# A hybrid attention and DeltaNet layer: the order of attention pieces, and which PSUM banks the middle projections use

## The chip, the cores and the metric

The kernel runs on one core of one Trainium2 chip. Its engines are TensorE (PE, with the weight loads PEld shown apart), VectorE (DVE), ScalarE (ACT), GpSimd (POOL) and SyncE (SP), whose queue issues all the DMAs here. The metric is the device time of one execution in microseconds (us). Shown are the median of several runs and, apart from them, one execution that was profiled.

## The reference

One layer of an encoder for 1024 tokens of width 1024, in float32:

```python
h = rms_norm(x, g_mix_pre);  proj = h @ w_in
aq, ak, av, dqkv, dgate, dalpha, dbeta = split(proj)
attn_o = window_attention(rope(aq), rope(ak), av, sink)   # 8 heads, 2 kv heads, blocks of 128, +-128 tokens
dn_o   = gated_deltanet(dqkv, dgate, dalpha, dbeta)       # 4 heads of 128, two directions, gated per-head norm
x = x + rms_norm(concat(attn_o, dn_o) @ w_out, g_mix_post)
c = cross_attention(rms_norm(x, g_cross_pre), rms_norm(mem, g_mem), w_cq, w_ckv, w_co)  # 4 heads of 256, 256 memory tokens
x = x + rms_norm(c, g_cross_post)
x = x + rms_norm(swiglu(rms_norm(x, g_ffn_pre), w_gate_up, w_down), g_ffn_post)
```

The chunked delta rule is a recurrence over the sequence; the kernel walks it in 8 steps of 128 tokens, for both directions at once.

## The kernel before, in words

Large products are made of three matmuls: each operand is split (`split`, L100) into a rounded part, written by ScalarE (L103), and a remainder, written by VectorE or GpSimd (L104), and the product of the two remainders is left out. Weights come through the pool `wp`: a load into `wraw`, then `whi` and `wlo`, each with two buffers (`load_w`, L119).

A planner orders the instructions of each engine when the program is built. It takes the program's order as priority, simulates the engines, and at each moment puts in what is ready; `load_w` raises its priority by 300 instructions (`AHEAD`). Tiles of one name in a pool share that name's buffers and get them in the order in which the program asks. On the chip each engine works through its list in the planned order, and so does the SP queue.

The mixer is written out as three lists of letters that `issue` (L729) walks.
- `ORDER_1` makes the DeltaNet's queries, keys and values and what the scans need of them.
- `ORDER_2` (L38) makes the rest: `L` are the last levels of the triangular inverses, `A` the attention projections, `V` the attention values, `G` the gate projections (`gate_proj`, L777), `W` calls `next_windows`.
- `ORDER_3` (L39): `M` normalises the memory tokens (`memory_norm`, L917), `s01` is one step of the scans of both head pairs (`scan`, L795), `K` one of eight column blocks of the memory keys (`next_keys`, L941), `V` one half of the memory values.

The window attention is cut into 16 pieces, one per block of 128 queries and kv group g (`window`, L632); pieces 0 to 7 belong to group 0. The first half of a piece makes four heads' scores on the PSUM tiles `psw`, the softmax, and the normalised probabilities `sc`. The second half transposes them (`ptw`) and multiplies by the values (`pow`). Both draw on two banks of the pool `pw`. One call of `next_windows` (L703) begins two pieces and finishes the two begun before them; nine calls make all 16. With the first piece of a group it calls `window_keys` (L696), which loads that group's keys into a `wraw` buffer (`kraw`) and splits them into `khi` (two buffers) and `klo` (one buffer).

The scans, the memory norm (`ptm`), the memory keys (`pck`) and the memory values (`pcv`) share the five PSUM banks of the pool `pc` (L792). The memory norm loads its two tiles `mt` into `wraw` buffers, and uses `whi` buffers (`mjk`) for the squares.

After the mixer, PSUM is three pools: `pg3` with four banks, `pn3` and `px3` with two each (L995 to L997). `mid_gemm` (L1034) multiplies 512 tokens by a 1024x1024 matrix, in two halves of 512 columns; each half is four tiles of 128 tokens, one bank each, and four blocks of the inner dimension. A bank is read out by ScalarE (L1055, the square sum) and VectorE (L1056, times the gain). At its end it adds the residual, stores the sum, and scales it by its own inverse root mean square into `xr` (L1072) for the next norm, whose transposes are `ptn`. It is called four times: twice for `w_out` (L1095, L1097) and twice for `w_co` (L1183, L1197), once per half of the tokens.

Between them stand the query projections (`cross_q`, tiles `pcq` in `pg3`) and the cross attention (`cross_attention`, L1121), once per token half. For each of four heads it makes scores `pcs` in two tiles of `px3`, their maxima and exponentials, transposes `pct` in `pn3`, and the product with the values `pco` in two tiles of `px3`, whose result replaces the queries. `w_co` then multiplies that result.

Of the kernel before, what the change touches and what calls it, by code (L numbers as in the profile page):

```python
# [13 lines left out]
AF = mybir.ActivationFunctionType  # L14
ALU = mybir.AluOpType
# [8 lines left out]
NT = S // P  # L24
# [10 lines left out]


ORDER_1 = ("k0 k1 E0 K0 U0 E1 K1 U1 S0 q0 v0 q1 C0 v1 E2 C1 k2 E3 k3 q2 K2 U2 v2 K3 U3 S1 q3 C2 v3 C3 B0 B1").split()
ORDER_2 = "L0 L1 A4 V A0 A1 G0 G1 L2 L3 W W W A2 A3 G2 G3 W".split()  # L38
ORDER_3 = ("M " + "s01 W K " * 5 + "s01 K " * 3 + "s01 V V").split()  # L39


_NAMES = ["ident", "mUi", "mLi", "m5", "m6", "band0", "band1", "band2", "mU", "mL", "ones"]
# [34 lines left out]
def tile_hybrid_block(  # L77
# [6 lines left out]
    nc = tc.nc  # L84
    x, mem, out = x[0], mem[0], out[0]
    w_in, w_out, w_cq, w_ckv, w_co = w_in[0], w_out[0], w_cq[0], w_ckv[0], w_co[0]
# [100 lines left out]
    d_x1 = dram.tile([S, D], F32, name="d_x1")  # L187
    d_x2 = dram.tile([S, D], F32, name="d_x2")
# [443 lines left out]
    def window(n, g):  # L632

        tok = slice(n * P, (n + 1) * P)
        k0, k1 = max(n - 1, 0), min(n + 1, NT - 1) + 1
        nb = k1 - k0
        w = nb * P
        band = C[:, _AT["band0"] - C0 + (k0 - n + 1) * P:][:, 0:w]

        khi, klo = (t[:, k0 * P:k1 * P] for t in keys[g])  # L640
        qr = tw.tile([P, 4, P], F32, tag="qr", name="qr", bufs=1)
        for r in range(2):
            nc.sync.dma_start(qr[64 * r:64 * r + 64], d_q[256 * g:256 * g + 256, tok].rearrange("(h e) t -> e h t", h=4))
        qs = tw.tile([P, 4, P], F32R, tag="qs", name="qs")
        nc.scalar.copy(qs, qr)
        nc.gpsimd.tensor_tensor(qs[64:128], qr[64:128], f32(qs[64:128]), ALU.subtract)

        m4 = tw.tile([P, 4], F32, tag="m4", name="m4")
        ssum = tw.tile([P, 4], F32, tag="ssum", name="ssum")
        pr = []  # L650
        for hh in range(4):
            pp = pw.tile([P, 512], F32, tag="pw", name="psw")
            for i, kk in enumerate((khi, klo)):
                nc.tensor.matmul(pp[:, 0:w], qs[:, hh, :], kk, start=(i == 0), stop=(i == 1))
            sc = tw.tile([P, 384], F32, tag="sc", name="sc", bufs=8)
            nc.vector.tensor_tensor_reduce(out=sc[:, 0:w], in0=pp[:, 0:w], in1=band, scale=0.125,
                                           scalar=sink[:, 4 * g + hh:4 * g + hh + 1], op0=ALU.add, op1=ALU.max,
                                           accum_out=m4[:, hh:hh + 1])
            pr.append(sc)
        nm = tw.tile([P, 4], F32, tag="nm", name="nm")  # L660
        nc.vector.tensor_scalar(nm, m4, -1.0, None, ALU.mult)
        for hh in range(4):
            nc.scalar.activation(pr[hh][:, 0:w], pr[hh][:, 0:w], AF.Exp, bias=nm[:, hh:hh + 1],
                                 accum_out=ssum[:, hh:hh + 1])
        es = tw.tile([P, 4], F32, tag="es", name="es")
        nc.gpsimd.tensor_tensor(es, sink[:, 4 * g:4 * g + 4], m4, ALU.subtract)
        nc.scalar.activation(es, es, AF.Exp)
        nc.vector.tensor_tensor(es, es, ssum, ALU.add)
        nc.vector.reciprocal(es, es)
        for hh in range(4):  # L670
            if g * NT + n < 8:
                nc.vector.tensor_scalar(pr[hh][:, 0:w], pr[hh][:, 0:w], es[:, hh:hh + 1], None, ALU.mult)
            else:
                nc.scalar.mul(pr[hh][:, 0:w], pr[hh][:, 0:w], es[:, hh:hh + 1])
        yield
        po = pw.tile([P, 4, P], F32, tag="pow", name="pow", bufs=1)
        for j in range(nb):
            pp = pw.tile([P, 512], F32, tag="pw", name="ptw")
            for hh in range(4):
                nc.tensor.transpose(pp[:, hh * P:(hh + 1) * P], pr[hh][:, j * P:(j + 1) * P], ident)  # L680
            ph = tw.tile([P, 512], F32R, tag="ph", name="ph")
            pl = tw.tile([P, 512], F32R, tag="pl", name="pl")
            split(ph, pl, pp)
            for i, pe_ in enumerate((ph, pl)):
                nc.tensor.matmul(po.rearrange("p h t -> p (h t)"), vhl[:, k0 + j, g].rearrange("p r e -> p (r e)"), pe_,
                                 start=(j == 0 and i == 0), stop=(j == nb - 1 and i == 1))
        ao = tw.tile([P, 4, P], F32, tag="ao", name="ao", bufs=1)[0:64]
        nc.scalar.copy(ao, po[64:128])
        nc.vector.tensor_tensor(ao, po[0:64], ao, ALU.add)
        nc.sync.dma_start(d_mix[g * 256:(g + 1) * 256, tok].rearrange("(h e) t -> e h t", e=64), ao)  # L690
# [307 lines left out]
    L0 = ExitStack()  # L998
# [14 lines left out]
    def turn_norm(xn, gname, his, los, pin=False):  # L1013

        for k in range(KT):
            pt = pn.tile([P, 512], F32, tag="pn", name="ptn")
            for j in range(4):
                t = nc.tensor.transpose(pt[:, j * P:(j + 1) * P], xn[j][:, k * P:(k + 1) * P], ident)
                if pin and k + j == 0:
                    tc.keep_in_program_order(t)  # L1020
            split(his[:, k, :], los[:, k, :], pt, gain(gname, k))
# [9 lines left out]

    PG, PN, PX = (pg, "pg"), (pn, "pn"), (px, "px")

    def mid_gemm(tz, act, w, gp, res, dst, hf, between=None, banks=([PG] * 4, [PX] * 2 + [PG] * 2)):  # L1034


        zs = [tz.tile([P, D], F32, tag="z", name="z", bufs=4) for _ in range(4)]
        sss = [tz.tile([P, 2], F32, tag="zss", name="zss", bufs=8) for _ in range(4)]
        for ch in range(2):
            cs = slice(ch * 512, (ch + 1) * 512)  # L1040
            if ch and between:
                between()

            pp = [q_.tile([P, 512], F32, tag=t_, name="pmg") for q_, t_ in banks[ch]]
            for kp in range(4):
                whi, wlo = load_w(w[kp * 256:(kp + 1) * 256, cs], 2, 512)
                for t in range(4):
                    tt = slice(t * P, (t + 1) * P)
                    for kk in range(2):
                        k = 2 * kp + kk  # L1050
                        for i, (w_, a) in enumerate(((whi, 0), (whi, 1), (wlo, 0))):
                            nc.tensor.matmul(pp[t], act[a][:, k, tt], w_[:, kk, :], start=(k == 0 and i == 0),  # L1052
                                             stop=(k == KT - 1 and i == 2))
            for t in range(4):
                nc.scalar.activation(zs[t][:, cs], pp[t], AF.Square, accum_out=sss[t][:, ch:ch + 1])  # L1055
                nc.vector.tensor_tensor(zs[t][:, cs], pp[t], gp[:, cs], ALU.mult)  # L1056
        xn = []
        for t in range(4):
            tok = slice(hf * HALF + t * P, hf * HALF + (t + 1) * P)
            z = zs[t]  # L1060
            xr = tz.tile([P, D], F32, tag="xr", name="xr", bufs=XR)
            nc.sync.dma_start(xr, res[tok, :])
            rs = tz.tile([P, 1], F32, tag="prs", name="prs", bufs=4)
            nc.gpsimd.tensor_scalar(rs, sss[t][:, 1:2], sss[t][:, 0:1], D * EPS, ALU.add, ALU.add)
            nc.gpsimd.tensor_tensor(rs, rs, mhalf[:, 0:1], ALU.pow)
            nc.vector.scalar_tensor_tensor(z, z, rs, xr, ALU.mult, ALU.add)
            nc.sync.dma_start(dst[tok, :], z)
            s2 = tz.tile([P, 1], F32, tag="ps2", name="ps2", bufs=4)
            nc.scalar.activation(xr, z, AF.Square, accum_out=s2)
            r2 = tz.tile([P, 1], F32, tag="pr2", name="pr2", bufs=4)  # L1070
            rstd_of(r2, s2, 1.0 / D, EPS)
            nc.vector.tensor_scalar(xr, z, r2, None, ALU.mult)  # L1072
            xn.append(xr)
        return xn

# [4 lines left out]
    L1 = ExitStack()  # L1080
# [11 lines left out]
                              .rearrange("(k p) t -> p k t", p=P))  # L1092
            split(mxT[hf][0][:, k2, :], mxT[hf][1][:, k2, :], raw[:, k2, :])
    LR.close()
    xn0 = mid_gemm(tz, mxT[0], w_out, gp, x, d_x1, 0, banks=([PG] * 4, [PX] * 2 + [PN] * 2))  # L1095
    h2T = [[opB.tile([P, KT, HALF], F32R, tag=b1, name=b1), opB_first[2]]]
    xn1 = mid_gemm(tz, mxT[1], w_out, gp, x, d_x1, 1, between=lambda: turn_norm(xn0, "cross", *h2T[0], pin=True))  # L1097
    h2T.append(operand(opA, "s0"))
    turn_norm(xn1, "cross", *h2T[1])

# [92 lines left out]
    for k in range(KT):  # L1193
        pt = turned_k(xn, k)
        nc.scalar.activation(raw[:, k, :], pt, AF.Identity, scale=gain("ffn", k))
        split(x1h[:, k, :], x1l[:, k, :], raw[:, k, :], eng=nc.gpsimd)
    xn = mid_gemm(tz, q1, w_co, gp, d_x1, d_x2, 1)  # L1197
    T2, T4 = (blocks(t) for t in operand(opB, "s1"))
    T1, T3 = (blocks(t) for t in operand(opB, "s2"))
    for k in range(HK):  # L1200
# [355 lines left out]
```

## Time and profile before

| what | value |
|---|---|
| median of 3 runs | 1556.27 us (1555.42 to 1558.12) |
| the profiled execution's own time | 1553.82 us |
| its span, first to last instruction | 1551.8 us |
| mean granted TensorE clock | 0.992 |
| scans, memory keys, window pieces | about 290 to 574 us of the span |
| `w_out` products, cross attention, `w_co` products | about 550 to 903 us |

The profile is of one execution. A row of the timeline gives start and length in us, engine, line, operation, written and read tiles, shapes and count; in square brackets stands how long the engine was idle before and what ended that. A row of a group gives the total, a mean in ns, and the idle time before the group with what ended it. A row of a tile's view gives durations (min/median/max in ns) and the first and last start. Rows of windows are explained where they stand.

### The profile page before, as it was taken

The page shows a single profiled execution, that of the slowest core. Times are in us where ns is not written, and L with a number is a line of the kernel's source. Part 1 is how long each engine was busy: PE and PEld are TensorE (multiplying, and loading weights), DVE is VectorE, ACT ScalarE, POOL GpSimd, SP SyncE. Part 2 cuts the span into 40 slices and gives each one's busy share as a digit, 9 for nine tenths or more (in the row PEclk, how much of TensorE's full clock was granted, in tenths as well). Part 3 has the DMA queues.
Part 4 walks back from the last instruction along what each step waited for, and adds up shares of the span by engine and source line. Part 5 has one row for each costly group of instructions (what it writes and reads, how often), then busy time and mean ns, then how long its engine had stood idle before and what let it go on. Part 6 is the DMA issues. An engine that isn't in the chain of part 4 may idle for free.

```text
span 1551.8 us, 21044 instructions
## 1 busy us (share of the span) xinstructions
PE 1488.0 (96%) x7451; PEld 1248.9 (80%) x7451; DVE 1074.3 (69%) x1728; ACT 740.3 (48%) x1522; POOL 379.9 (24%) x364
## 2 busy tenths in 40 slices
PE   6999999998999999999987999999999999999997
PEld 5888888787989788888876887888888888888786
DVE  6868999686888766643444577776867554696665
ACT  5578732557467764443333664332323332354532
POOL 2020210111256103433000531443433432000021
PEclk9999999999999999999999999999999999999999
DMA  6244575856996755542210554344433334853354
GB/s 205 75 117 136 158 189 158 190 173 187 328 303 210 246 196 180 179 155 77 68 41 27 188 192 144 116 128 129 156 118 113 105 106 150 290 188 98 102 175 164
DMA packets 264710, 242.95 MB, mean 157 GB/s; under 512 B 33800, under 2 KB 203677, under 8 KB 264605
## 3 DMA queue, kind: packets, MB, share of 16 engines
q1 hardware_dynamic: 264605, 241.62, 50.0%
q8 instruction: 58, 0.95, 0.3%
q14 instruction: 47, 0.39, 0.1%
HBM read 172.07 MB, written 66.88 MB: 154 GB/s over the span
## 4 chain that ended last, share of the span: by engine, by line
PE 70%; DVE 7%; DMA 5%; ACT 5%; issue 2%; SPq 1%; POOL 1%; DVEq 0%; POOLq 0%; ACTq 0%
PE pmg L1052 11%; PE pD L1227 8%; PE pE L1227 8%; PE pA L1227 7%; PE pdX L1417 6%; PE pcq L261 5%; PE pdA L1417 4%; PE pB L1227 4%; PE psc L809 3%; PE pg L261 3%; PE pdD L1417 2%; PE pco L1159 2%; PE pcs L1133 2%; PE pck L949 1%; PE pdX L1510 1%
## 5 line engine op out<-in xcount | busy, mean ns | idle before, releaser
L103 ACT CAST whi<-wraw 128x1024 fp32r<-128x1024 f32 x108 | 113.6, 1052 | 176.6 <-PE pmg L1052 50.1
L261 PE MATMUL pg<-hlo,whi 128*128 128x512 f32 x352 | 139.7, 397 | 0.0
L261 PE MATMUL pg<-hhi,whi 128*128 128x512 f32 x352 | 139.3, 396 | 0.0
L261 PE MATMUL pg<-hhi,wlo 128*128 128x512 f32 x352 | 138.8, 395 | 0.0
L104 POOL TENSOR_TENSOR wlo<-wraw,whi 128x1024 fp32r<-128x1024 f32 x38 | 92.5, 2435 | 184.1 <-ACT whi L103 176.6
L104 DVE TENSOR_TENSOR wlo<-wraw,whi 128x1024 fp32r<-128x1024 f32 x70 | 87.1, 1245 | 71.9 <-ACT whi L103 64.4
L1052 PE MATMUL pmg<-whi,b 128*128 128x512 f32 x384 | 117.0, 393 | 1.1 <-DVE b L104 0.9
L1227 PE MATMUL pA<-s,whi 128*128 128x512 f32 x352 | 109.3, 392 | 1.0 <-ACT m L1244 1.0
L1052 PEld LDWEIGHTS pmg<-whi,b 128*128 128x128 f32 x384 | 71.5, 188 | 16.3 <-DVE b L104 1.4
L261 PEld LDWEIGHTS pg<-hhi,whi 128*128 128x128 f32 x352 | 66.6, 189 | 13.6 <-ACT hhi L103 0.2
L1417 PE MATMUL pdX<-dhl,whi 128*128 128x512 f32 x264 | 76.0, 390 | 1.5 <-DVE zv L1472 0.7
L1227 PEld LDWEIGHTS pA<-s,whi 128*128 128x128 f32 x352 | 65.5, 188 | 14.7 <-ACT m L1244 1.5
L261 PEld LDWEIGHTS pg<-hhi,wlo 128*128 128x128 f32 x352 | 66.5, 189 | 13.0
L261 PEld LDWEIGHTS pg<-hlo,whi 128*128 128x128 f32 x352 | 66.5, 189 | 12.9
L1304 POOL TENSOR_TENSOR act<-act,up 128x512 f32<-128x512 f32 x33 | 50.1, 1519 | 87.6 <-DVE up L1303 47.3
L1052 PE MATMUL pmg<-wlo,b 128*128 128x512 f32 x192 | 71.1, 391 | 0.0
L103 ACT CAST whi<-araw 128x1024 fp32r<-128x1024 f32 (+1 forms) x36 | 35.4, 982 | 71.0 <-PE pdX L1417 27.6
L1227 PE MATMUL pA<-s,wlo 128*128 128x512 f32 x176 | 68.7, 391 | 0.0
L104 DVE TENSOR_TENSOR wlo<-araw,whi 128x1024 fp32r<-128x1024 f32 (+1 forms) x36 | 40.8, 1133 | 38.9 <-ACT whi L103 38.9
L286 DVE SCALAR_TENSOR_TENSOR acc<-cp,cols,acc 128x1024 f32<-128x1024 f32 x48 | 62.1, 1295 | 0.1
L1276 POOL TENSOR_TENSOR sr<-wraw 128x512 f32<-128x512 f32 x22 | 31.0, 1410 | 126.5 <-DMA wraw<-in_w_gate_up_dram 125.2
L1447 POOL TENSOR_SCALAR frs<-sq 128x1 f32<-128x1 f32 x8 | 12.0, 1498 | 195.9 <-ACT jk L1436 194.9
(414 smaller groups left out, 4107.8 us busy)
## 6 DMA issues: line engine op xcount, KB each, us to landing
wraw<-in_w_gate_up_dram SPq DMA_DIRECT2D x52, 512.0 KB, 3.8
kv<-d_kv SPq DMA_DIRECT2D x32, 512.0 KB, 6.7
wraw<-in_w_in_dram SPq DMA_DIRECT2D x22, 512.0 KB, 4.7
b<-in_w_down_dram SPq DMA_DIRECT2D x20, 512.0 KB, 6.9
araw<-d_as SPq DMA_DIRECT2D x20, 512.0 KB, 3.7
pz<-d_pz SPq DMA_DIRECT2D x32, 256.0 KB, 5.2
wraw<-in_w_ckv_dram SPq DMA_DIRECT2D x16, 512.0 KB, 9.2
wraw<-in_w_out_dram SPq DMA_DIRECT2D x16, 512.0 KB, 3.7
```

What stands on the lines that cost most here:

```text
L103: nc.scalar.copy(hi, src)
L104: (eng or nc.vector).tensor_tensor(lo, src, f32(hi), ALU.subtract)
L261: nc.tensor.matmul(p_, w[:, k, :], ah[a][:, k, :], start=(k == 0 and i == 0), stop=(k == nk - 1 and i == 2))
L286: nc.vector.scalar_tensor_tensor(acc, cp[:, t:t + S], taps[t], acc, ALU.mult, ALU.add)
L809: nc.tensor.matmul(out[:, d, h, :], lt[:, d, h, :], rt[:, d, h, :], start=True, stop=True)
L1052: nc.tensor.matmul(pp[t], act[a][:, k, tt], w_[:, kk, :], start=(k == 0 and i == 0), stop=(k == KT - 1 and i == 2))
L1133: nc.tensor.matmul(pp[:, t2_, :], q[a][:, ct, tt], kr_[b_][:, ct, :], start=(j == 0 and i == 0), stop=(j == 1 and i == 2))
L1159: nc.tensor.matmul(po, vr_[a][:, kt, cs], pts[kt][b_], start=(kt == 0 and i == 0), stop=(kt == 1 and i == 2))
L1227: nc.tensor.matmul(out_, w[a][:, k, :], xx[b_][:, k, :], start=(start and k == 0 and i == 0), stop=(k == HK - 1 and i == 2), skip_group_ch ...
L1276: nc.gpsimd.tensor_tensor(s[0], b_[:, 0:HK], b_[:, HK:], ALU.add)
L1304: nc.gpsimd.tensor_tensor(o_, o_, up, ALU.mult)
L1417: nc.tensor.matmul(banks[t], a[:, k - k0, tt], w, start=(first and k == 0 and i == 0), stop=(k == NB - 1 and i == 2), skip_group_check=not ...
```

## The change

- `ORDER_2` makes five calls of `next_windows` instead of four, the last two ahead of the gate projections `G2 G3`; `ORDER_3` makes four instead of five, one after each of the first four scan steps.
- The probabilities of pieces 8 to 11 are normalised by VectorE (L672) instead of ScalarE (L674).
- `mid_gemm` takes all its banks from `pg3` unless told otherwise. The first `w_out` product keeps its banks (`px3`, `pn3`), and the second is now told to use `px3` as it did; the two `w_co` products stay in `pg3` for both halves.
- The last scaling of `mid_gemm` runs on ScalarE unless `vec` is set. It is set in the first `w_out` and the second `w_co` product.

```diff
-ORDER_2 = "L0 L1 A4 V A0 A1 G0 G1 L2 L3 W W W A2 A3 G2 G3 W".split()
-ORDER_3 = ("M " + "s01 W K " * 5 + "s01 K " * 3 + "s01 V V").split()
+ORDER_2 = "L0 L1 A4 V A0 A1 G0 G1 L2 L3 W W W A2 A3 W W G2 G3".split()
+ORDER_3 = ("M " + "s01 W K " * 4 + "s01 K " * 4 + "s01 V V").split()
...
-            if g * NT + n < 8:
+            if g * NT + n < 12:
                 nc.vector.tensor_scalar(pr[hh][:, 0:w], pr[hh][:, 0:w], es[:, hh:hh + 1], None, ALU.mult)
             else:
                 nc.scalar.mul(pr[hh][:, 0:w], pr[hh][:, 0:w], es[:, hh:hh + 1])
...
-    def mid_gemm(tz, act, w, gp, res, dst, hf, between=None, banks=([PG] * 4, [PX] * 2 + [PG] * 2)):
+    def mid_gemm(tz, act, w, gp, res, dst, hf, between=None, banks=([PG] * 4, [PG] * 4), vec=False):
...
-            nc.vector.tensor_scalar(xr, z, r2, None, ALU.mult)
+            if vec:
+                nc.vector.tensor_scalar(xr, z, r2, None, ALU.mult)
+            else:
+                nc.scalar.activation(xr, z, AF.Identity, scale=r2)
...
-    xn0 = mid_gemm(tz, mxT[0], w_out, gp, x, d_x1, 0, banks=([PG] * 4, [PX] * 2 + [PN] * 2))
+    xn0 = mid_gemm(tz, mxT[0], w_out, gp, x, d_x1, 0, banks=([PG] * 4, [PX] * 2 + [PN] * 2), vec=True)
...
-    xn1 = mid_gemm(tz, mxT[1], w_out, gp, x, d_x1, 1, between=lambda: turn_norm(xn0, "cross", *h2T[0], pin=True))
+    xn1 = mid_gemm(tz, mxT[1], w_out, gp, x, d_x1, 1, banks=([PG] * 4, [PX] * 2 + [PG] * 2),
+                   between=lambda: turn_norm(xn0, "cross", *h2T[0], pin=True))
...
-    xn = mid_gemm(tz, q1, w_co, gp, d_x1, d_x2, 1)
+    xn = mid_gemm(tz, q1, w_co, gp, d_x1, d_x2, 1, vec=True)
```

## The prediction

> **What bounds the kernel.** I read the page's busy shares first, then the windows, to find where the busiest engine is not busy.
>
> ```profile
> PE 1488.0 (96%) x7451; PEld 1248.9 (80%) x7451; DVE 1074.3 (69%) x1728; ACT 740.3 (48%) x1522; POOL 379.9 (24%) x364
> PE   6999999998999999999987999999999999999997
> ```
>
> TensorE is busy in 1488.0 of 1551.8 us, and the change neither adds nor removes a matmul. What it can win or lose is the 64 us in which TensorE is idle, and the matmuls that run slowly beside such holes. The windows show the largest hole after the start-up:
>
> ```profile
> 780.00:800.00 20.00, 19.80 (x102) 16.43 (x101) 10.96 (x18) 8.51 (x22) 0.00 (x0) 1.00 0.15 53
> 801.38:839.38 38.00, 25.64 (x133) 19.67 (x133) 18.14 (x38) 13.21 (x38) 0.00 (x0) 0.91 0.00 0
> ```
>
> (Columns: length; busy PE, PEld, DVE, ACT, POOL with counts; granted clock; DMA share; GB/s.) From 801.38 to 839.38 TensorE idles for 12.4 us, the clock falls to 0.91 and no byte is moved. The timeline says what runs there:
>
> ```profile
> 802.31 3.13 PE L1133 MATMUL pcs<-kr,b 128*128 128x256 f32 x24 [0.93 <-DVE b L104]
> 804.04 0.69 DVE L1135 TENSOR_REDUCE cmx<-pcs 128x2 f32<-128x512 f32 x1 [1.19 <-PE pcs L1133]
> 807.12 0.63 PE L1149 MATMUL pct<-ident,cpr 128*128 128x128 f32 x4 [1.68 <-ACT cpr L1140]
> 809.00 1.07 ACT L103 CAST cph<-pct 128x512 fp32r<-128x512 f32 x2 [1.51 <-PE pct L1149]
> 813.45 1.07 ACT L103 CAST b<-pco 128x512 fp32r<-128x512 f32 x2 [3.38 <-PE pco L1159]
> 814.07 1.29 DVE L104 TENSOR_TENSOR b<-pco,b 128x512 fp32r<-128x512 f32 x2 [3.16 <-ACT b L103]
> ```
>
> This is one head of the second cross attention. Scores, maximum, exponential, transposes, values and the split of the result follow one another, each waiting for the last. Three such heads run with nothing beside them. Why nothing? The chain in order of time gives the pieces before and after:
>
> ```profile
> 712.13 2.79 PE pco L1159 x12
> 743.33 2.87 PE pcs L1133 x24
> 757.56 0.91 PE pmg L1052 x4
> 766.52 2.87 PE pcs L1133 x24
> 776.00 0.87 PE pct L1149 x8
> 839.38 26.80 PE pmg L1052 x117
> 885.65 17.47 PE pmg L1052 x77
> ```
>
> The first product with `w_co` (`pmg`) filled the earlier heads from 757.56 on, as the query projection had before it. It then stopped, and its second half of columns came at 839.38, after the last head. Its inputs were there long before:
>
> ```profile
> 790.37 0.60 ACT L1055 ACTIVATE z<-pmg 128x512 f32<-128x512 f32 x1 [2.18 <-PE pmg L1052]
> 792.99 1.07 ACT L103 CAST whi<-wraw 128x1024 fp32r<-128x1024 f32 x1
> 795.24 0.68 DVE L1056 TENSOR_TENSOR z<-pmg,gpost 128x512 f32<-128x512 f32 x1
> ```
>
> The weights' cast ends at 794.1, and the last of the four `pg3` banks is read out at 795.9. What was missing is the bank: tiles 0 and 1 of that half come from `px3`, whose two banks the heads use (`pcs`, `pco`). A `px3` bank lies empty between a head's exponentials and its values, and `pmg` does not take it: a pool's buffers go out in program order, and the heads stand first. The DMA queue agrees: it moves nothing, because the raw weights' buffers are not returned.
>
> **Part 1: the `w_co` products stay in `pg3` (L1034, L1183, L1197).** The second half no longer queues behind the heads. At full rate a head costs TensorE 2.87 + 0.87 + 2.79 = 6.53 us; three cost 19.6 of the 38.0 us. So at most 18.4 us can be filled, the slow matmuls at clock 0.91 counted with it. Filler: the half has 96 matmuls at 17.47/77 = 0.227 us, 21.8 us. With filler at hand a head took 766.52 - 743.33 = 23.2 us, so the planner may use 16.7 us of it per head and run out after 1.3 heads, leaving 1.7 x 6.1 = 10.4 us unfilled: the lower end is a gain of 8. But the product of the second token half can start on the rows of the heads already done, as the first did at 757.56, a head and a half before its last: three of four k blocks, 72 x 0.227 = 16.3 us more. Together 38 us for an 18.4 us hole. I take -17.0, near the upper end, 0.5 us per head being lost in hand-overs. What follows 839 is TensorE-bound (the slices of the page's PE line read 9 from there to the last but one), so the gain carries through. The price: with four banks, a chunk's first matmul waits for the bank of the chunk before to be read out. The cover is the 18 matmuls of the three other tiles, 4.1 us, against 0.6 on ScalarE and 0.68 on VectorE. I cost it at nothing; if both engines are late by 2 us at the three boundaries, it is 6.
>
> [...]
>
> **Part 2: the last scaling of `mid_gemm` (L1072) goes to ScalarE in the mixer's second product and the first `w_co` product, four 128x1024 tiles each.**
>
> ```profile
> 655.99 0.75 DVE L1072 TENSOR_SCALAR xr<-z,pr 128x1024 f32<-128x1024 f32 x1
> 657.18 2.86 DVE L1072 TENSOR_SCALAR xr<-z,pr 128x1024 f32<-128x1024 f32 x1 [0.44 <-POOL pr L162]
> 657.12 2.37 POOL L104 TENSOR_TENSOR wlo<-wraw,whi 128x1024 fp32r<-128x1024 f32 x1
> PE ptn L1018 <- DVE xr L1072: 2.5, 2, 1.5
> L1069 ACT ACTIVATE xr<-z 128x1024 f32<-128x1024 f32 x16 | 16.9, 1057 | 9.3 <-DVE z L1066 8.4 <-issue 0.8
> ```
>
> VectorE needs 0.75 us, but 2.86 beside a GpSimd subtraction, and TensorE waited 2.5 us in all for it. An activation of that size takes 1.06. In the mixer the wait goes, and what is late next is the GpSimd root before it: -2.0, between -2.5 and +1.2 (four tiles 0.31 slower each, unhidden). In `w_co` it lies under the heads: nothing. [...]
>
> **Part 3: the order.** `W` moves from behind `G3` to before `G2`, and a second `W` joins it from the scans; `ORDER_3` has one less. Each `W` issues on SP two query loads and a store per piece, on GpSimd a subtraction and a small difference per piece. They pass two weight loads and four gate stores, which nothing needs until step 4. The pieces run in a chain of their own two score banks and are late already (the eighth piece's scores end near 425, five scan steps in), so their order costs nothing. But the fifth `W` also calls `window_keys(1)`, and its buffer matters:
>
> ```profile
> 300.32 0.37 SPq L126 DMA_DIRECT2D wraw<-in_w_in_dram  x1
> 329.54 1.05 ACT L103 CAST whi<-wraw 128x1024 fp32r<-128x1024 f32 x1 [0.82 <-DMA d_pz<-Z]
> L699 SPq DMA_DIRECT2D kraw<-d_k x4: 474/566/1809, 249.1 to 374.0; - x4
> L103 ACT CAST khi<-kraw x2: 1045/1050/1054, 278.2 to 385.9; 128x1024 fp32r<-128x1024 f32 x2
> L104 DVE TENSOR_TENSOR klo<-kraw,khi x2: 1221/1223/1225, 284.5 to 425.5; 128x1024 fp32r<-128x1024 f32 x2
> L921 SPq DMA_DIRECT2D mt<-in_mem_dram x2: 514/520/527, 314.5 to 335.7; - x2
> L924 ACT ACTIVATE mjk<-mt x2: 1046/1052/1058, 364.2 to 365.4; 128x1024 f32<-128x1024 f32 x2
> L934 PE MATMUL ptm<-ident,mt x16: 272/272/327, 369.5 to 372.6; 128*128 128x128 f32 x16
> DMA to landing us min/median/max: 4.5/4.5/4.5
> ```
>
> The second `kraw` takes one of the two `wraw` buffers at 374 and keeps it until 425.5, since `klo` has one buffer, free only when piece 7's scores are done. Now it takes it near 285, ahead of G2, G3 and both `mt` tiles of the memory norm, which all go through the other. G2 and G3 lose nothing: G3's weights are issued at 300.32 and cast at 329.54 only, so a load some 15 us later is still in time. The first `mt` comes at about 335 instead of 314.5, unnoticed. The second waits for the first's transposes (369.5): issue 370.5, landed 375 to 380 (4.5 us, or 10 in the crowded queue), and 7.5 us more to the last transpose (365.4 to 372.9). What waits for that:
>
> ```profile
> 373.42 0.54 SPq L126 DMA_DIRECT2D wraw<-in_w_ckv_dram  x1
> 385.32 0.59 PE L949 MATMUL pck<-mT,whi 128*128 128x256 f32 x2 [2.19 <-ACT whi L103]
> 385.71 1.91 PE L809 MATMUL psc<-S,kv 128*128 128x128 f32 x8
> ```
>
> The first memory-key weights are loaded right after the norm (373.42), their product starts at 385.32, and the second scan step's first matmul comes only behind it, since both draw on the five `pc` banks in program order. That load moves to 382.5 to 388, a shift of 9 to 15 us; I take 11. Bounds: all of it idle, +15; or nothing lost and 2.1 us recovered at the tail (below, 520 to 540), where the pieces end earlier. TensorE has attention pieces meanwhile, and 2.19 us of waiting is there already: +4, a third of the shift.
>
> **Part 4: pieces 8 to 11 are normalised on VectorE.**
>
> ```profile
> L672 DVE TENSOR_SCALAR sc<-sc,es 128x384 f32<-128x384 f32 (+1 forms) x32 | 10.7, 399 | 0.2
> 460.00:480.00 20.00, 18.72 (x152) 17.91 (x151) 18.57 (x48) 15.93 (x52) 12.33 (x17) 1.00 0.75 215
> 520.00:540.00 20.00, 17.91 (x80) 13.44 (x78) 14.20 (x25) 15.97 (x28) 2.57 (x3) 0.91 0.95 349
> ```
>
> Sixteen times 0.399 = 6.4 us go to an engine busy for 18.57 of 20 us there. Bounds 0 and 6.4; I take +1, as TensorE is nearer its limit.
>
> **Sum.** -17.0 - 2.0 + 4 + 1 = -14.0. The profiled execution took 1553.82 us, so 1539.8; the median of the runs is 2.45 above it, which gives 1542.
>
> **Rivals.** *A, slower: the memory norm waits for `kraw`.* If the first `mt` is not returned by its own transposes, the second waits for 425.5 + 1.2; adding 4.5, 7.5, and the 11.9 us from 373.42 to 385.32, the second step starts near 451 instead of 385.7. With about half of those 65 us filled by attention pieces (an estimate), +32: 1556 - 18 + 32 = 1570. It decides where the transposes of the first tile stand behind those of the second. Against it: they need only the first tile. *B: the late start is dear*, 12 to 15 us, with part 4 at 3 to 6: 1552. For it: at 18.72 of 20 (460 to 480) TensorE leaves a late scan little room to catch up. *C: the hole stays or moves*, since TensorE's fixed order puts the filler where its banks are not read out: no gain from part 1, 6 at the boundaries, part 3 as above: 1565. For it: the planner's spacing of 23.2 us per head, against 38.0/3 = 12.7 unfilled. Against it: the same filling left 0.2 us idle from 780 to 800.
>
> **How the numbers follow.** Likeliest 0.68 (its own range 1534 to 1551), B 0.13, A 0.10, C 0.06, anything else 0.03. Differences under 0.2%, about 3 us, are what a measurement of this kernel can't tell from none. Faster: the likeliest and most of B, 0.79; same 0.06; slower 0.15. The range 1533 to 1560 takes in the best ends (-18.4 - 2.5 - 2.1) and B; it leaves out A and most of C.
>
> **What would show it.** Part 1: `pmg` between the heads from 798 to the last head, TensorE above 19.5 of 20 and the clock at 1.00 there, DMA moving. Part 2: no wait of `ptn` L1018 on VectorE. Part 3: the second `mt` load behind the first `ptm`, the first `pck` 9 to 15 us later. I am wrong if `pmg` still starts after the last `pco`, or the first `pck` comes after 430.

## The result and the profile after

The changed kernel took 1576.76 us (median of four runs, 1575.26 to 1579.62), the kernel before 1555.85 beside it: a ratio of 1.0139 with a 95% interval of 1.0113 to 1.0165, some 21 us slower, where 1542 was forecast. The profiled execution took 1578.04 us. One of the twelve runs of e9 below took 5784 us and is left out of its ratio.

First the page of the changed kernel: busy shares, then TensorE and its granted clock in 40 slices of 39.4 us.

```profile
PE 1500.9 (95%) x7451; PEld 1256.3 (80%) x7451; DVE 1078.3 (68%) x1736; ACT 740.9 (47%) x1514; POOL 371.9 (24%) x364
PE   6999999898799969999999999999999999999997
PEclk9999999999699989999999999999999999999999
```

The number of matmuls is the same, but they were busy for 12.9 us longer, and the span grew by 24.4. Two slices are low in TensorE's row and in its clock's, the eleventh (394 to 433) and the fifteenth (552 to 591). The low slices of the kernel before, the 21st and 22nd, are gone. So the scans got worse and the cross attention better. The tile views of a few landmarks give the size of both. Rows of a tile's view end with the first and last start; the first three are of the kernel before, the next four of the changed one:

```profile
L1052 PE MATMUL pmg<-whi,s x128: 387/389/478, 552.4 to 599.0; 128*128 128x512 f32 x128
L1133 PE MATMUL pcs<-kr,b x192: 277/283/387, 658.3 to 830.6; 128*128 128x256 f32 x192
L1227 PE MATMUL pA<-s,whi x352: 387/389/499, 903.0 to 1324.5; 128*128 128x512 f32 x176
```

```profile
L949 PE MATMUL pck<-mT,whi x128: 277/282/419, 428.5 to 551.1; 128*128 128x256 f32 x128
L1052 PE MATMUL pmg<-whi,s x128: 387/389/497, 596.3 to 641.4; 128*128 128x512 f32 x128
L1137 PE MATMUL pcs<-kr,b x192: 277/283/366, 700.6 to 889.3; 128*128 128x256 f32 x192
L1231 PE MATMUL pA<-s,whi x352: 387/389/499, 928.1 to 1349.5; 128*128 128x512 f32 x176
```

| first start of | before | after | later by |
|---|---|---|---|
| `pck`, memory keys (second scan step) | 385.3 | 428.5 | 43.2 |
| `pmg`, first `w_out` product | 552.4 | 596.3 | 43.9 |
| `pcs`, first cross scores | 658.3 | 700.6 | 42.3 |
| `pA`, behind the last `w_co` product | 903.0 | 928.1 | 25.1 |
| end of the span | 1551.8 | 1576.2 | 24.4 |

So 43.9 us were lost up to the scans' end, 1.6 won back before the first cross scores, and 17.2 between the first cross scores and the end of `w_co`.

**Where the 17.2 came from.** The stretch that held the hole, in the changed kernel (windows, columns as in the prediction), and the chain of waits from 802 on:

```profile
801.38:839.38 38.00, 37.80 (x197) 31.82 (x196) 19.29 (x32) 14.57 (x36) 0.00 (x0) 1.00 0.20 64
```

```profile
802.17 4.81 PE pmg L1052 x21
806.98 2.87 PE pcs L1137 x24
809.85 6.15 PE pmg L1052 x27
817.34 2.77 PE pmg L1052 x12
820.12 2.34 PE pco L1163 x10
...
846.40 2.87 PE pcs L1137 x24
849.27 7.28 PE pmg L1052 x32
```

The whole stage lies some 42 us later here, so the window alone would not do. The chain shows what changed: `pmg` stands between the scores (`pcs`) and the values (`pco`) of each head, as `pcq` did for the earlier ones.

**Where the 43.9 was lost.** Tile views of the key group and of the memory norm in the changed kernel:

```profile
L699 SPq DMA_DIRECT2D kraw<-d_k x4: 537/770/1051, 248.8 to 287.9; - x4
L104 DVE TENSOR_TENSOR klo<-kraw,khi x2: 1214/1220/1226, 284.5 to 408.2; 128x1024 fp32r<-128x1024 f32 x2
L921 SPq DMA_DIRECT2D mt<-in_mem_dram x2: 554/576/597, 337.9 to 411.3; - x2
L934 PE MATMUL ptm<-ident,mt x16: 270/421/477, 371.4 to 421.9; 128*128 128x128 f32 x16
```

The second `kraw` is loaded at 287.9 and is released by the split of `klo` at 408.2. The second `mt` is issued at 411.3 (335.7 before). The timeline (TensorE, VectorE and SyncE's queue) has the whole chain:

```profile
371.35 0.60 PE L934 MATMUL ptm<-ident,mt 128*128 128x128 f32 x4
...
407.34 0.41 PE L654 MATMUL psw<-klo,qs 128*128 128x256 f32 x1
408.21 1.21 DVE L104 TENSOR_TENSOR klo<-kraw,khi 128x1024 fp32r<-128x1024 f32 x1
411.25 0.55 SPq L921 DMA_DIRECT2D mt<-in_mem_dram  x1
419.49 2.82 PE L934 MATMUL ptm<-ident,mt 128*128 128x128 f32 x12 [1.34 <-DVE mt L927]
428.50 0.63 PE L949 MATMUL pck<-mT,whi 128*128 128x256 f32 x2
428.93 2.18 PE L809 MATMUL psc<-S,kv 128*128 128x128 f32 x14
```

Only four of the first tile's eight transposes ran at 371.35; the other four stand among the twelve at 419.49. TensorE's written order, with the tiles' numbers (`mt_4227` is the first tile, `mt_4236` the second), says why:

```
MATMUL ptm_4245<-mt_4227      (at 371.35, and one each of ptm_4254, ptm_4263, ptm_4272)
...
MATMUL ptm_4245<-mt_4236      (from 419.49 on)
MATMUL ptm_4245<-mt_4227
MATMUL ptm_4245<-mt_4236
MATMUL ptm_4254<-mt_4236
MATMUL ptm_4254<-mt_4227
```

The loop in `memory_norm` (`for i` over two columns of 128, inside it `for j` over the two tiles) writes each PSUM tile alternately from the first and the second `mt`, and the planner kept the writes into one PSUM tile in that order. So the first `mt` cannot be given back before the second is there, and the second can only get the buffer that `kraw` holds.

**What TensorE did meanwhile.** Windows of the kernel before, then of the changed one: 360 to 440, 520 to 600, and 360 to the first `pmg`:

```profile
360.00:440.00 80.00, 74.08 (x552) 68.73 (x551) 63.91 (x175) 47.59 (x105) 22.59 (x19) 0.98 0.98 294
520.00:600.00 80.00, 77.31 (x355) 62.48 (x354) 52.05 (x75) 54.95 (x98) 6.28 (x9) 0.98 0.68 233
360.00:552.40 192.40, 178.89 (x1255) 163.03 (x1254) 154.09 (x387) 131.02 (x327) 67.86 (x78) 0.97 0.84 262
```

```profile
360.00:440.00 80.00, 61.97 (x315) 49.41 (x314) 57.68 (x142) 47.99 (x115) 17.91 (x20) 0.83 0.63 184
520.00:600.00 80.00, 65.12 (x376) 55.00 (x375) 45.77 (x84) 44.19 (x100) 16.05 (x24) 0.91 0.70 229
360.00:596.30 236.30, 201.30 (x1296) 176.73 (x1296) 173.09 (x414) 134.94 (x334) 64.19 (x78) 0.91 0.71 225
```

And a row from the waits of TensorE in the changed kernel (us in total, times, longest):

```profile
PE pcv L965 <- ACT whi L103: 9.4, 4, 5.9
```

From 360 to the first `pmg` TensorE idles for 35.0 us in place of 13.5, and is busy for 201.30 in place of 178.89: 21.5 and 22.4, together the 43.9. The busy time grew while the mean clock was 0.91 in place of 0.97 and 41 more matmuls fell into the stretch; how much belongs to which is not worked out. From 394 to 419 TensorE ran nothing but pieces. So they were used up sooner: their last values (`pow`) start at 551.3, against 572.0 before the change, though the scans end 44 us later. None were left for the end, where the memory-value products (`pcv`) wait 9.4 us for their weights, and 14.9 of the 80 us from 520 on are idle (2.7 before). The pieces did not make good the late scan.

### The profile page after: what moved, and what is told of

It reads as the page before. It is cut to its first block, busy times and chain, and to the rows that moved or that the text cites. A ratio compares the mean times of both kernels' runs of the same rounds, so it can differ in the third digit from the quotient of the medians.

```text
span 1576.2 us, 21052 instructions
## 1 busy us (share of the span) xinstructions
PE 1500.9 (95%) x7451; PEld 1256.3 (80%) x7451; DVE 1078.3 (68%) x1736; ACT 740.9 (47%) x1514; POOL 371.9 (24%) x364
## 4 chain that ended last, share of the span: by engine, by line
PE 65%; DVE 5%; DMA 3%; ACT 2%; issue 1%; SPq 0%; DVEq 0%; POOL 0%; POOLq 0%; ACTq 0%
PE pmg L1052 10%; PE pD L1231 7%; PE pE L1231 7%; PE pA L1231 7%; PE pcq L261 6%; PE pdX L1421 5%; PE pdA L1421 4%; PE pB L1231 4%; PE psc L809 3%; PE pdX L1514 2%; PE pdD L1421 2%; PE pcs L1137 1%; PE pco L1163 1%; PE pck L949 1%; PE pow L685 1%
## 5 line engine op out<-in xcount | busy, mean ns | idle before, releaser
L103 ACT CAST whi<-wraw 128x1024 fp32r<-128x1024 f32 x108 | 113.4, 1051 | 159.5 <-PE pmg L1052 34.3
L1421 PEld LDWEIGHTS pdX<-dhl,whi 128*128 128x128 f32 x264 | 49.3, 188 | 12.7 <-ACT dhl L103 1.1
```

Source lines behind the costliest of these rows:

```text
L103: nc.scalar.copy(hi, src)
L1421: nc.tensor.matmul(banks[t], a[:, k - k0, tt], w, start=(first and k == 0 and i == 0), stop=(k == NB - 1 and i == 2), skip_group_check=not ...
```

## The experiments

Two theories stood against each other. T: the write order inside the PSUM tiles keeps the first `mt`, so that the norm waits for `kraw` and the split of `klo`. R: pieces taken ahead of the scans leave the scans nothing to fill with, whenever the norm ends. Each ratio is against runs of the kernel before on the same chip, with its 95% interval.

### e1_row_order: the wait removed, all else as changed

```
-            for i in range(2):
-                k = 2 * k2 + i
-                for j in range(2):
+            for j in range(2):
+                for i in range(2):
+                    k = 2 * k2 + i
                     nc.tensor.transpose(pt[:, i, j * P:(j + 1) * P], mn[j][:, k * P:(k + 1) * P], ident)
```

> The changed kernel, with one thing different: in the memory norm the transposes of one PSUM tile are written in the order of the input tiles (both of the first mt, then both of the second), where they alternated before. Theory T (the write order inside a PSUM tile keeps the first mt's buffer until the second mt is there, so the second waits for kraw and the split of klo at 408.2): the first mt is now returned after its eight transposes near 372, the second mt is loaded at 372 to 376 instead of 411.3, the first pck starts at 392 to 400 instead of 428.5, and the time falls by 29 to 37 us, to 1540 to 1548. Theory R (the pieces ahead of the scans leave the scans nothing to fill with, whenever the norm ends): the first pck comes earlier as well, but the hole behind the scans (9.6 us of TensorE idle from 560 to 600) stays or grows, and the time stays above 1562.

Measured: 1542.54 us, 0.9922 (0.9900 to 0.9944), 34.2 us below the changed kernel. The tile views of `mt` and `pck` in this kernel:

```profile
L921 SPq DMA_DIRECT2D mt<-in_mem_dram x2: 332/431/530, 338.9 to 373.8; - x2
L949 PE MATMUL pck<-mT,whi x128: 278/283/386, 394.7 to 514.8; 128*128 128x256 f32 x128
```

The second `mt` is issued at 373.8, right behind the first's transposes, and the first `pck` comes at 394.7. `klo` is split at 424.3, and nothing waits for that now. The order strings are the changed ones, so R falls: the place of the pieces is not what cost 34 us.

### e2_order_alone, e3_order_undone, e14_order_undone_again, e4_banks_alone: the parts

e2 is the kernel before with the two changed order strings. e3 and e14 are the same kernel: the changed one with the old strings. e4 is the kernel before with this:

```
-banks=([PG] * 4, [PX] * 2 + [PG] * 2)):            # default of mid_gemm, used by both w_co products
+banks=([PG] * 4, [PG] * 4)):                        # the mixer's calls name their banks as before
```

> The kernel before with part 3 alone (both order strings), banks, scaling and the pieces' multiply as before. Theory T: the second mt is again issued behind the split of klo near 410, the scans end some 42 us later than before, and as the hole in the second cross attention stays, the whole shift arrives at the end: 1593 to 1601. If instead the order costs only the 21 us by which the changed kernel is slower, and the other parts are worth nothing: 1574 to 1580.

> The changed kernel with both order strings as before, that is parts 1, 2 and 4 without part 3. Theory T with the prediction's terms (-17, -2, +1): second mt and first pck as in the kernel before (335.7, 385.3), no hole of TensorE between 790 and 840, 1536 to 1541. If the products' gain in the changed kernel came only because the scans were late (rival C: the filler stays behind the heads): 1553 to 1562.

> The same kernel as e3_order_undone (parts 1, 2 and 4 with the order of the kernel before), in more runs beside e8_rows_in_before and e15_kraw_in_whi. If its 1534.3 was right, 1532 to 1537 and a ratio of 0.985 to 0.989; if it was luck of four runs, 1538 to 1543.

> The kernel before with part 1 alone: both w_co products take all four banks from pg3 in both halves; everything else as before. By the prediction's part 1: pmg stands between the heads from 798 to 838, TensorE is busy for more than 37 of the 38 us from 801.38 to 839.38, and the time is 17 us lower, 1537 to 1541 (bounds 1537 to 1548). Rival C (hole stays or moves, four banks make the products wait at their boundaries): 1553 to 1562.

Measured: e2 1590.60, 1.0220 (1.0185 to 1.0256); e3 1534.33, 0.9875 (0.9836 to 0.9914); e14 1535.60, 0.9885 (0.9867 to 0.9903); e4 1539.80, 0.9903 (0.9872 to 0.9935). The order alone costs 35 us, a little under what T expected, and e3 is 2 us under its range; in e2 the first `pck` comes at 430.1, and the second `mt` is issued at 412.8. Without the new order the change wins 18 to 21 us, most of it by the banks, 15.7. The window of the old hole in e4, and a row of its waits:

```profile
801.38:839.38 38.00, 38.00 (x195) 32.27 (x194) 25.26 (x37) 18.78 (x40) 9.57 (x16) 1.00 0.33 116
```

```profile
PE pmg L1052 <- ACT b L103: 0.4, 2, 0.2
```

In e3 and e4 the stage lies within 10 us of where it lay before the change; TensorE is busy for 36.69 and 38.00 of the 38 us, and the clock is at 1.00 in both. The last row is the only wait of `pmg` among TensorE's waits in e4: 0.4 us for a head's result, none for a bank. Rival C falls. e3 and e14 beat both kernels of this case.

### e10_keys_early and e7_one_W_ahead: the held buffer or the pieces

In e10 a new item stands before `G2`, which calls `window_keys(1)`; the W that called it no longer does. No piece moves. In e7 the fourth W is moved before `G2`, and the keys stay where they were.

```
e10: -ORDER_2 = "... W W W A2 A3 G2 G3 W"      e7: -ORDER_2 = "... W W W A2 A3 G2 G3 W"
     +ORDER_2 = "... W W W A2 A3 Y G2 G3 W"        +ORDER_2 = "... W W W A2 A3 W G2 G3"
     +"Y": lambda: window_keys(1)
```

> The kernel before with only the second key group's load and split (window_keys(1)) called ahead of G2 and G3; no piece moves, and the scans' steps keep their five W. Theory T (the held buffer is the cause, not the pieces' order): the second mt waits again for the split of klo, which comes when the scores of piece 7 are done, 408 to 426; the first pck starts 35 to 58 us later than in the kernel before, and nearly all of it arrives at the end: 1588 to 1610. Theory R (the loss comes from pieces taken ahead of the scans): no piece was moved, so no loss: 1553 to 1560.

> The kernel before with only the fourth W moved from behind G3 to before G2 (pieces 6 and 7); the fifth W, which loads the second key group, stays in the scans. Theory T: second mt and first pck as before (335.7 and 385.3, within 2 us), no loss: 1552 to 1559. Theory R: pieces taken ahead of G2, G3 and the memory norm delay them or empty the scans: 1560 or more.

Measured: e10 1583.69, 1.0183 (1.0157 to 1.0209); e7 1555.10, 1.0001 (0.9985 to 1.0016). Tile views of e10:

```profile
L104 DVE TENSOR_TENSOR klo<-kraw,khi x2: 1211/1218/1226, 284.9 to 407.1; 128x1024 fp32r<-128x1024 f32 x2
L921 SPq DMA_DIRECT2D mt<-in_mem_dram x2: 338/432/527, 338.3 to 408.3; - x2
L949 PE MATMUL pck<-mT,whi x128: 277/283/387, 424.2 to 543.7; 128*128 128x256 f32 x128
L685 PE MATMUL pow<-pl,vhl x44: 390/476/796, 329.7 to 534.6; 128*128 128x512 f32 x44
```

The early keys alone cost 28.8 us, with no piece moved; the fourth W moved alone (pieces 6 and 7) costs nothing. e2, which moves a fifth W as well, is some 6 us slower than e10 by the ratios, but the intervals overlap. e10's time is below the range expected: of the 38.9 us by which `pck` came later, 28.8 arrived. The last row shows what T had left open: the last of the pieces' values starts at 534.6, in the kernel before at 572.0, though their place in the program is the old one. They are used up because the scans wait, so R has cause and effect the wrong way round.

### e15_kraw_in_whi: the wait removed in another way

```
-raw = wp.tile([P, S], F32, tag="wraw", name="kraw")
+raw = f32(wp.tile([P, S], F32R, tag="whi", name="kraw")) if g else wp.tile([P, S], F32, tag="wraw", name="kraw")
```

> The changed kernel, write order untouched, but the second kraw takes its buffer from the whi ring instead of the wraw ring, so both mt have a wraw buffer although klo is still waiting for the scores of piece 7. Theory T: second mt at 336 to 345 as in the kernel before, first pck at 385 to 395, the 34 us go: 1534 to 1545. If the wait of the second mt was not the cause, but the pieces and keys ahead of G2, G3 were: 1565 or more.

Measured: 1541.85, 0.9928 (0.9911 to 0.9946), with the transposes as they were. Tile views:

```profile
L921 SPq DMA_DIRECT2D mt<-in_mem_dram x2: 382/454/527, 340.3 to 363.8; - x2
L949 PE MATMUL pck<-mT,whi x128: 277/283/365, 398.6 to 516.1; 128*128 128x256 f32 x128
```

The time is as T had it, though the second `mt` came 19 us later than expected, and `pck` 3.6. The timeline of e15 says why: the cast of G3's weights comes at 360.94 (331.95 in the changed kernel), having waited for TensorE to be done with an earlier `whi`, of which `kraw` now holds one. The split that frees the raw weights starts at 362.51, and the second `mt` is issued into their buffer at 363.85. Two removals of one wait give 34.2 and 34.9 us. A buffer of its own for the second `kraw` wasn't tried.

### e8, e10b, e11, e12: what is left of part 3

e1 is 7 to 8 us above e3 and e14, though its norm waits for nothing but its own buffer. Is that the later start, or the rewritten loop itself? e8 is the kernel before with the loop of e1; e10b is e10 with that loop; e11 is e3 with it; e12 is e11 with the order of e7.

> The kernel before with only the second key group's load ahead of G2 and G3 (as in e10_keys_early), and the norm's transposes in the order of the input tiles. No piece moves. Theory T: the second mt waits for the first's eight transposes only, the first pck comes 8 to 12 us later than in the kernel before. If a late scan is paid in full (as e1_row_order against e3_order_undone, 8.2 us for a shift of 8.5): 1563 to 1567. If the remaining 8.2 us come from the pieces' place and not from the shift: 1554 to 1558. If a third of the shift is paid, as the prediction had it: 1558 to 1560.

> Parts 1, 2 and 4 with the order of the kernel before, and the norm's transposes in the order of the input tiles. In this order both mt have a buffer early, so the write order should be worth nothing: the same as e3_order_undone, 1532 to 1537. If the norm ends earlier by it as well: 1529 to 1532.

> As e11_rows_and_order_undone, with the fourth W ahead of G2 as well (the move that e7_one_W_ahead made in the kernel before, which cost nothing there). 1532 to 1537; lower than e11_rows_and_order_undone only if pieces 6 and 7 fill TensorE where it waits at the start of the scans.

> The kernel before with only the norm's transposes in the order of the input tiles. Both mt have a buffer early there, so nothing waits for the write order itself. If e11_rows_and_order_undone is slower than e3_order_undone (1543.8 against 1534.3) because the write order reshuffles the scans' and pieces' order in the planner: 3 to 10 us slower than before, 1558 to 1565. If that difference is only the spread of four and six runs: 1553 to 1558.

| pair (both with the rewritten loop, except the last) | `pck` later by | times | cost |
|---|---|---|---|
| e10b against e8 | 393.2 - 387.5 = 5.7 | 1561.23, 1.0038 (1.0024 to 1.0051); 1559.53, 1.0032 (1.0018 to 1.0047) | 1 by the ratios |
| e1 against e11 | 394.7 - 389.8 = 4.9 | 1542.54, 0.9922; 1543.82, 0.9920 (0.9899 to 0.9941) | none |
| e12 against e11 | 385.6 - 389.8 = -4.2 | 1542.98, 0.9916 (0.9893 to 0.9939); 1543.82 | none |
| e15 against e14 | 398.6 - 388.5 = 10.1 | 1541.85, 0.9928; 1535.60, 0.9885 | 6 |

The loop costs 5 us by itself in the kernel before (e8), where nothing waits for it, and 5 (by the ratios) to 8 in e11 against e14; I had expected the same time for e11, and so for e12. That is as much as lies between e1 and e14. The timeline of e8 shows a place where it is lost, the first `w_out` product (first ScalarE, then TensorE):

```profile
566.15 1.90 ACT L103 CAST vr<-mvr 128x2048 fp32r<-128x2048 f32 x1 [7.27 <-DMA mvr<-d_mv]
570.26 3.78 PE L1052 MATMUL pmg<-whi,s 128*128 128x512 f32 x8 [3.30 <-ACT whi L103]
```

In the planned order ScalarE waits 7.3 us for the load of the memory values (`mvr`) ahead of the next `w_out` weights, and TensorE then waits 3.3 us for those. From 560 to 580 it is busy for 16.70 of 20 us at a clock of 0.83; in the kernel before it was 20.00 at 1.00. In e11 a wait for such a cast takes 2.1 us, which e14 has not. The pieces are ordered otherwise too. Rows of e11's, then of e14's tile views of `pow`, the pieces' values:

```profile
L685 PE MATMUL pow<-pl,vhl x44: 389/475/793, 330.0 to 585.3; 128*128 128x512 f32 x44
```

```profile
L685 PE MATMUL pow<-pl,vhl x44: 389/436/501, 328.5 to 567.6; 128*128 128x512 f32 x44
```

The memory keys stand alike (`pck` from 389.8 to 509.9 and from 388.5 to 510.9), but the pieces end 17.7 us later. Why the planner orders so much otherwise for moved transposes stays open.

The first two pairs of the table are a balance, not a shift without effect. In e10b and e1 the first `pmg` comes 8.2 and 2.6 us later than in e8 and e11, but the pieces end 13.3 and 8.1 us earlier, and the first cross scores come at the same time and 4.2 us earlier. e10b's time lies between the ranges written for it. What is left of part 3 is thus nothing that shows where the norm is 5 to 6 us late. It is 6 us in e15, where the norm is 10 us late, but there the gate projections are 10 us late as well: their last matmul starts at 367.4, against 357.3 in e14.

### e9_act_alone and e5_mul_alone: parts 2 and 4

e9 is the kernel before with the `vec` argument and its branch, e5 with `< 12` for `< 8`.

> The kernel before with part 2 alone: the last scaling of mid_gemm on ScalarE in the mixer's second product and in the first w_co product. By the prediction: the waits of ptn for xr on VectorE go (2.5 us in all), 1.0 to 2.5 us faster, 1553 to 1555. If ScalarE's longer 1.06 us is what is late next: 1556 to 1557.

> The kernel before with part 4 alone: pieces 8 to 11 are normalised on VectorE. By the prediction: 0 to 6.4 us slower, about 1, so 1556 to 1558. If ScalarE was the later of the two engines in the scans: 1 to 4 us faster, 1552 to 1555.

Measured: e9 1553.80, 0.9990 (0.9975 to 1.0006); e5 1553.37, 0.9994 (0.9977 to 1.0010). Neither can be told from no change. In e9 the wait of TensorE for the scaled rows is 0.6 us where the prediction's row of the kernel before has 2.5, as this row of its waits says:

```profile
PE ptn L1193 <- ACT xr L1075: 0.6, 1, 0.6
```

That is a wait behind the `w_co` product, which the kernel before did not have; the one in the mixer (L1018) is gone. The changed kernel and e14 have neither. On ScalarE a scaling took 1.15 us in e9 (median), where the prediction put 1.06.

## Why the prediction was wrong, and where it was right

**Part 1, right.** Forecast -17.0; alone (e4) it gave 15.7. In e4 the stretch from the first cross scores to `pA` is 14.6 us shorter than in the kernel before (230.1 against 244.7). The 17.2 of the changed kernel hold part 2 as well. `pmg` stands between the heads, of which the scores at 806.98 and 846.40 are two steps apart, 19.7 us each. The clock is at 1.00 and the DMA queue moves weights (64 GB/s). Four banks cost nothing at the chunk boundaries: e4 runs the products on four banks and is faster (0.9903), and the 0.4 us that its `pmg` waited were for a head's result. The heads used the four banks of `px3` and `pn3` meanwhile.

**Part 2, right in mechanism.** The wait went, forecast -2.0, measured -1.6 by the ratio of e9, between -3.9 and +0.9. The two waits of the kernel before lie at 660.10 and 663.76, behind the first cross scores at 658.3. So they belong to the stretch up to `pA`: it takes 227.6 us in e14, which has parts 1 and 2, and 230.1 in e4, a difference of 2.5. The shift that fell from 43.9 to 42.3 before the first cross scores is not part 2's: in e2 and e10, which lack part 2, it falls too, from 42.5 to 39.9 and from 34.3 to 31.0.

**Part 4, not told apart.** Forecast +1; e5 gives -0.9, between -3.6 and +1.6. The 6.4 us more on VectorE did not show; the upper bound of the prediction lies outside the interval.

**Part 3, wrong.** These steps held: the second `kraw` near 285 (285.75 and 287.95 in the queue), the first `mt` at about 335 (337.9), hardly any harm to G2 and G3 (G3's weights are cast at 331.95, against 329.54), the pieces' order costing nothing (e7, for the fourth W). The step that failed is "the second waits for the first's transposes (369.5)", with "against it: they need only the first tile" under rival A. In its place the second `mt` waited for the split of `klo` and was issued at 411.3 instead of 370.5; the first `pck` came 43.2 us later instead of 9 to 15, and the term of +4 was +35 alone (e2). Each transpose does need only one tile, but the queue's order decided (four of the first tile's ran at 371.35, the other four from 419.49 on), and that order came from the kernel's own loop: the writes of one PSUM tile alternate between the two `mt`. The profile of before could not show it, since both tiles were there, but the row of `ptm` (369.5 to 372.6 for all sixteen) did not show the opposite either. Rival A named this condition, and it was given 0.10. The mark for it, a first `pck` after 430, was set a little too late: it came at 428.5.

**The size of rival A.** It gave 1570, from a shift of 65 us with half of it filled. The shift was 43.2, since TensorE, with nothing but pieces to run, reached the eighth piece's scores at 407.3, not at 425. And it was paid in full, 43.9 at the first `w_out` product: filling early with pieces only emptied the scans' end (TensorE idle for 14.9 us from 520 to 600, 2.7 before). The two errors cancel in part, 1570 against 1576.8.

**The sum without the wait.** The forecast of 1542 is what e1 and e15 gave, 1542.5 and 1541.9. That is partly luck. The predicted +4 for a shift of 11 us was in truth 1 us or nothing for shifts of 5.7 and 4.9 (e10b, e1), and e1's 5 to 8 us over the kernel without the new order are what the rewritten loop costs elsewhere. e15 pays 6 us for a shift of 10.1, but with the gate projections late as well. So the size of that term stays open. The parts without part 3 were forecast at -18 and gave -18 to -21 (e14, e3). The best kernel of this study is therefore the change without its order strings: 0.9885 (0.9867 to 0.9903) of the kernel before, about 41 us under the changed one.

## What to carry to other kernels

In this kernel a buffer of a ring came back when its last reader had run in the queue's order, not when that reader's inputs were there: the first `mt` was there at 371.35, and four of its eight transposes ran from 419.49 on. So before a tile is moved ahead of others in its ring, read which instructions release each buffer and what stands before them in the queue, down to the loop that alternates writes into one PSUM tile. When independent work fills a stall, ask what that work was to cover later. And try the parts of a bundle apart: here one cost 35 to 41 us (e2, and the changed kernel against e14) and hid that the others had won 18.

## What the runs showed that was not expected

The clock fell to half, and no wait in the 14 us ahead was longer than 1.48 us. Windows of 4 us of the changed kernel while only pieces ran, and two rows of its timeline, the second with TensorE's longest wait since 390:

```profile
400.00:404.00 4.00, 2.13 (x8) 1.07 (x8) 1.55 (x5) 3.55 (x11) 0.23 (x2) 0.82 0.22 66
404.00:408.00 4.00, 3.62 (x12) 2.75 (x13) 3.96 (x14) 0.79 (x2) 0.00 (x0) 0.50 0.00 2
412.00:416.00 4.00, 3.56 (x12) 2.35 (x10) 2.04 (x9) 1.37 (x6) 0.00 (x0) 0.50 0.67 195
416.00:420.00 4.00, 2.15 (x8) 1.77 (x9) 2.17 (x7) 2.25 (x4) 1.75 (x3) 0.50 0.01 3
```

```profile
399.82 0.49 PE L685 MATMUL pow<-ph,vhl 128*128 128x512 f32 x1
403.12 0.79 PE L685 MATMUL pow<-ph,vhl 128*128 128x512 f32 x1 [1.48 <-ACT ph L103]
```

From 404 to 420 the granted clock is 0.50, and a `pow` matmul of the same form takes 0.63 to 0.80 us in place of 0.39 to 0.50 from 389 to 401, though TensorE is busy for 3.6 of 4 us in two of these windows and its longest wait between 390 and 404 was 1.48 us. What brought the 0.50 on is not shown.

So a busy share of 3.6 of 4 us at a clock of 0.50 is not work at the full rate here, and the prediction, which counted on pieces as filler between 360 and 440, had no term for a clock of 0.83. Whether the low clock cost time of its own is not shown. In the changed kernel TensorE was busy for 14.77 of the 20 us from 400 to 420 at a clock of 0.56. In e2, with the same wait, it was busy for 10.61 at 0.94, and its first `pck` comes 1.6 us later than the changed kernel's. In e10, with that wait as well, the clock was 0.50 from 400 to 416, and its first `pck` comes 4.3 us earlier.
